# Layer 1's scan on one core: odd pairs mirrored, two chains taking turns product by product, v's projection in pieces of six products

## The chip, the core and the metric

The kernel runs on one core of a Trainium2 chip. The metric is the device time of one execution in microseconds. TensorE (PE in the profile) multiplies and writes PSUM; VectorE (DVE) and ScalarE (ACT) read PSUM and do elementwise work; GpSimd (POOL) does elementwise work in SBUF; SyncE's queue (SP) issues DMAs.

## The reference, cut to what matters

The program is a trunk of two layers on 512 tokens of width 2048, in float32. Layer 0 is attention and a pooling mixer; the change leaves its arithmetic alone. Layer 1 is RWKV-7 time mixing with 32 heads of 64:

```python
def step(state, inp):
    r_t, w_t, k_t, v_t, kk_t, a_t = inp
    sa = jnp.einsum('bhvk,bhk->bhv', state, -kk_t)
    state = (state * w_t[:, :, None, :]
             + sa[..., None] * (kk_t * a_t)[:, :, None, :]
             + v_t[..., None] * k_t[:, :, None, :])
    return state, jnp.einsum('bhvk,bhk->bhv', state, r_t)
```

This recurrence runs over the 512 tokens for each head. Before it stand the projections of r, k, v and the gate; after it a group norm, the gate and the output projection.

## The kernel before, in words

The recurrence is worked in chunks of 64 tokens, 8 chunks for each head. Two heads make a pair `p`, 16 pairs in all, one head on partitions 0 to 63 and the other on 64 to 127. Ahead of the scan, `prep` (L756) writes for each pair the scaled vectors to DRAM: `AR` (per chunk 64 columns of "a", 64 of "r") and `BK` (per chunk 64 columns of "b", 64 of "k").

`scan` (L814) holds generators, one for each kind of work on one pair; a `next` issues one piece.

- `vproj` (L844): v's projection for the pair, 16 steps of three products 128x128 by 512 (`mm3`, L140, lines 142 to 144 in the profile, output `vps`), then a copy on ACT. It yields after each step: 16 pieces.
- `gprod` (L863): the chunk's products of BK and AR, masked by DVE into two tiles `Z` (L882), and the transposed BK in `BT`: 6 pieces.
- `lanes` (L912, 18 pieces, DVE almost alone: a serial inversion in blocks of 16, L928 and L929) and `levels` (L947, 5 pieces, four of which hold products, L963 and L973) make the chunk's inverse `U`. `vprep` (L892) fills `RS` with v, `post` (L1035, 6 pieces) is the group norm; its DVE line L1054 must be done before its transposes on PE, L1058.
- `chain` (L992): the serial part, 8 chunks of three steps. Step one: `xo` gets AR times the state M (L1002, one product with 128 output rows for "a" and "r" at once; the first chunk has none) and, on the 64 "a" rows, Z times RS for each head (L1004); DVE (L1006) and ACT (L1007) copy the a rows to `xs`. Step two: `sa` = U times xs (L1010, 64 output rows); DVE copies it to RS (L1011). Step three: `s1` = BT times RS (L1017, one head on the lower 64 output rows, one on the upper), from which DVE makes the next state M (L1026, L1028, two operations); then Z times RS on the 64 "r" rows of xo (L1030), which ACT copies to the output O (L1031).

In every pair "a" stands on the lower 64 output rows (`lo`) and "r" on the upper 64 (`hi`). A product whose output has 64 rows uses one half of TensorE's columns, lower or upper; all of these use all 128 rows of the array. A float32 product runs as two passes, so the profile counts two instructions for each call.

The order of TensorE's work is written by hand (L753); other engines are ordered by the framework. `slot` (L1117) runs two chains side by side, one pair in its last four chunks and the next pair in its first four: 12 rounds a slot, and in a round each chain gives one step, then come the pieces of other work that are due:

```python
for q in range(12):
    for c in chains:
        with tc.high_priority(offset=400):
            next(c)
    while todo and todo[0][0] < at + q + 1:
        next(todo.pop(0)[2])
```

`plan` (L1115) gives the pieces of each generator evenly spaced due times between two bounds (L31, in rounds). For slots 0 to 12 this makes one pattern of 12 rounds. By the bounds, v's 16 pieces fall on twelve rounds, ten of them alone and three times two in a row; gprod's products on rounds 0, 1, 3, 4, 6 and 7; levels' products on rounds 5, 7, 9 and 10; post's transposes on round 5, vprep's on round 11. Slot -1 holds one chain and slot 15 one; from the middle of slot 13 on v's pieces are gone, and pieces of the output projection (`project`, L1095, lines 488 to 490, output `y`) take their place.

Of the kernel before, what the change touches and what calls it, by code (L numbers as in the profile page):

```python
# [17 lines left out]
P = 128  # L18
# [16 lines left out]
class Kernel:  # L35
# [488 lines left out]
    def consts1(self, cp, tp):  # L524
        nc = self.nc
        f = lambda n, w=P: tp.tile([P, w], F32, name="c1" + n)

        mk = self.mk = cp.tile([P, P], F32, name="mk")
        nc.gpsimd.memset(mk, 1.0)
        nc.gpsimd.affine_select(mk[:64, :64], mk[:64, :64], [[1, 64]], ALU.is_gt, 0.0, base=0, channel_multiplier=-1)  # L530
        nc.gpsimd.affine_select(mk[:64, 64:], mk[:64, 64:], [[1, 64]], ALU.is_ge, 0.0, base=0, channel_multiplier=-1)
        nc.vector.tensor_copy(mk[64:, :], mk[:64, :])
# [223 lines left out]
    def prep(self, tp, p, r, hid, k_d, rn_d, ar_d, bk_d, bc_d):  # L756
# [35 lines left out]
        nc.vector.scalar_tensor_tensor(rn, k, col(self.hv["kk"]), rn, ALU.mult, ALU.mult)  # L792
        nc.vector.scalar_tensor_tensor(AR[:, :, 0, :], c8(rn), -2.0, Pi[:, :, 0:64], ALU.mult, ALU.mult)
        nc.vector.tensor_mul(AR[:, :, 1, :], c8(r), Pi[:, :, 1:])
        nc.sync.dma_start(ar_d[p], AR.rearrange("p a b c -> p (a b c)"))
        nc.vector.scalar_tensor_tensor(rn, ta, 1.0, rn, ALU.add, ALU.mult)
        nc.vector.tensor_mul(BK[:, :, 0, :], c8(rn), c8(iP))
        nc.scalar.activation(ta, ta, AF.Identity, scale=col(self.hv["ka"]), bias=col(self.hv["oka"]))
        nc.vector.tensor_mul(k, k, ta)
        nc.vector.tensor_mul(BK[:, :, 1, :], c8(k), c8(iP))  # L800
        nc.sync.dma_start(bk_d[p], BK.rearrange("p a b c -> p (a b c)"))
# [12 lines left out]
    def scan(self, ctx, xv, first, mp, ld, ar_d, bk_d, bc_d, g_d, m_d):  # L814
# [29 lines left out]
        def vproj(p):  # L844

            unit = lambda k0: self.wunit(
                Wv[k0 * P:(k0 + 4) * P, p * P:(p + 1) * P].rearrange("(k p) n -> p k n", p=P), 4, P,
                eng=nc.gpsimd if p > 1 else None)
            ws = first if p == 0 else [unit(0)]
            ps = pv.tile([P, S], F32, tag="v", name="vps")  # L850
            for k in range(NK):
                if k % 4 == 0:
                    wh, wl = ws.pop(0)
                    if k + 4 < NK and not ws:
                        ws.append(unit(k + 4))
                self.mm3(ps, wh[:, k % 4, :], wl[:, k % 4, :], xv[k][:, 0, :], xv[k][:, 1, :], k == 0, k == NK - 1)
                if k < NK - 1:
                    yield
            vT = sets[p]["vT"] = tp.tile([P, S], F32, tag="vT", name="vT")
            nc.scalar.copy(vT, ps)  # L860
            yield

        def gprod(p):  # L863
# [9 lines left out]
            for b in range(2):  # L873
# [7 lines left out]
                for h in range(2):  # L881
                    nc.vector.tensor_mul(Z[h][:, 4 * b:4 * b + 4, :], g[h], self.mk.unsqueeze(1).to_broadcast([P, 4, P]))  # L882
                yield
# [8 lines left out]
        def vprep(p):  # L892
# [6 lines left out]
            RS = s["RS"] = st.tile([P, 8, 2, 64], F32, tag="RS", name="RS", bufs=3)  # L899
            nc.gpsimd.memset(RS[lo], 0.0)  # L900
            yield
# [4 lines left out]
            for par, rows in ((0, lo), (1, hi)):  # L906
                nc.scalar.copy(RS[hi, par::2], g5[rows])
            yield
# [3 lines left out]
        def lanes(p):  # L912

            for q in range(4):
                r, c = slice(32 * q, 32 * q + 32), slice(32 * (q % 2), 32 * (q % 2) + 32)
                nc.gpsimd.tensor_mul(nd2[r, :, :16].rearrange("p t (b c) -> p c b t", b=2),
                                     sets[p]["Z"][q // 2][c, :, c].rearrange("p c (b t) -> p c b t", b=2),
                                     self.md[c, c].rearrange("p (b t) -> p b t", b=2)
                                     .unsqueeze(1).to_broadcast([32, 8, 2, 16]))
# [27 lines left out]
        def levels(p):  # L947
# [5 lines left out]
            N1 = tp.tile([P, 8, 64], F32, tag="N1", name="N1")  # L953
            nc.scalar.copy(N1[hi], sets[p]["Z"][1][lo, :, :64])
            N = sets[p]["Z"][0], N1
            yield
# [35 lines left out]
        def chain(p):  # L992

            s = sets[p]
            AR, RS, U, BT, Z = (s[n] for n in ("AR", "RS", "U", "BT", "Z"))
            O = s["O"] = tp.tile([P, 4, 2, 64], F32, tag="O", name="O", bufs=3)
            M = None
            for c in range(8):

                xo = pc.tile([P, 2, 64], F32, tag="c", name="xo")  # L1000
                if c:
                    mm(xo, AR[:, c].rearrange("p a b -> p (a b)"), M, start=True, stop=False)  # L1002
                for h in range(2):
                    mm(xo[lo, h, :], Z[h][:, c, :64], RS[:, c, h, :], start=c == 0 and h == 0, stop=h == 1)  # L1004
                xs = xsb[p % 2]
                nc.vector.tensor_copy(xs[lo, 0, :], xo[lo, 0, :])  # L1006
                nc.scalar.copy(xs[hi, 1, :], xo[lo, 1, :])  # L1007
                yield
                sa = po.tile([64, 2, 64], F32, tag="o", name="sa")
                mm(sa, U[:, c, :], xs, start=True, stop=True)  # L1010
                nc.vector.tensor_copy(RS[lo, c], sa)  # L1011
                yield
                Mn = None
                if c < 7:
                    s1 = po.tile([P, 64], F32, tag="o", name="s1")
                    for h in range(2):
                        mm(s1[half[h], :], BT[:, c, 64 * h:64 * h + 64], RS[:, c, h, :], start=True, stop=True)  # L1017
                    Mn = Ms[p % 2 * 2 + c % 2]
                    if c:
                        m0 = tp.tile([P, 2, 64], F32, tag="m0", name="m0", bufs=2)  # L1020
                        nc.scalar.activation(m0, M, AF.Copy, scale=self.pcs[:, p, c:c + 1])
                    for h in range(2):
                        hh = half[h]
                        pC = self.pcs[hh, p, c:c + 1]
                        if c:
                            nc.vector.scalar_tensor_tensor(Mn[hh, h, :], s1[hh, :], pC, m0[hh, h, :], ALU.mult, ALU.add)  # L1026
                        else:
                            nc.vector.tensor_scalar(Mn[hh, h, :], s1[hh, :], pC, None, ALU.mult)  # L1028
                for h in range(2):
                    mm(xo[hi, h, :], Z[h][:, c, 64:], RS[:, c, h, :], start=c == 0 and h == 0, stop=h == 1)  # L1030
                nc.scalar.copy(O[half[c % 2], c // 2], xo[hi])  # L1031
                M = Mn
                yield

# [84 lines left out]
        def slot(at, chains):  # L1119

            todo.sort(key=lambda x: x[0])
            for q in range(12):
                for c in chains:
                    with tc.high_priority(offset=400):
                        next(c)
                while todo and todo[0][0] < at + q + 1:
# [9 lines left out]
        def plan_pair(base, q, skip=0):  # L1136
# [11 lines left out]
        next(gp)  # L1148
        for q in range(7):
            next(v)  # L1150
        run(gp)
        la = lanes(0)
        for q in range(16):
            next(la)
            next(v, None)
        g1, v = gprod(1), vproj(1)
        next(g1)
        run(la)
        for q in range(6):
            next(g1)  # L1160
            next(v)
        run(vprep(0))
        la, l0 = lanes(1), levels(0)
        for q in range(10):
            if q % 2 == 0:
                next(l0, None)
            if q < 6:
                next(la)
            next(v)
        run(l0)  # L1170
# [115 lines left out]
```

## Time and profile before

| what | value |
|---|---|
| median of three runs | 2153.81 us |
| lowest and highest | 2153.8 and 2154.24 us |
| the profiled execution | 2158.38 us |
| its span, first to last instruction | 2156.7 us |
| mean granted TensorE clock (1 is 2.4 GHz) | 0.989 |

The profile is of one execution; 1.7 us of its time lie outside its span. The scan runs from about 1467 us to 1985 us of the span; slot 0 begins at 1490.5 us. A line of the timeline gives the start of the first instruction of a run of like ones, the time until the last of them ends, the engine, the line, out and in, rows and columns of the array (as 128*64), the operands and the count. Matmul ends are modelled and overlap; what a run of products costs is the distance from its start to the start of the next.

### The profile page before, as it was taken

To read this page: it belongs to the slowest core of one execution; us is meant where nothing else is said; L and a number is where in the kernel's file an instruction comes from. 1 tells how busy PE (TensorE), PEld (TensorE's weight loads), DVE (VectorE), ACT (ScalarE), POOL (GpSimd) and SP (SyncE) were. 2 spreads that over 40 slices of the span, in tenths; PEclk is the share of its full clock that TensorE was granted. 3 is DMA by queue.
4 is the path that set the end of the run, shared out by engine and by line. 5 is a ranking of instruction groups with operands and counts; after the bars stand their busy time and mean duration, and the time that the engine had idled before them with its cause. 6 is when DMAs were issued, how large, how long until landed. Compare 5 with 4: busy or idle time off the path is not lost.

```text
span 2156.7 us, 33268 instructions
## 1 busy us (share of the span) xinstructions
PE 2087.6 (97%) x12915; PEld 1688.5 (78%) x12915; DVE 1272.0 (59%) x2557; ACT 951.8 (44%) x1663; POOL 266.1 (12%) x333
## 2 busy tenths in 40 slices
PE   8999999999999989998999989999999999999997
PEld 7888888888888888777788768876777777767786
DVE  4334335444333368677767872276787877876346
ACT  3335435333221248455545662254555555554211
POOL 0000000000000000233000020022233233210003
PEclk9999999999999999999999999999999999999998
DMA  5322222333333353554466664321232332232633
GB/s 189 98 70 81 85 73 69 93 98 98 98 108 114 127 175 112 165 165 149 159 209 223 219 226 152 107 84 45 89 99 81 93 104 77 91 118 89 229 103 112
DMA packets 214029, 262.94 MB, mean 122 GB/s; under 512 B 15768, under 2 KB 161776, under 8 KB 213104
## 3 DMA queue, kind: packets, MB, share of 16 engines
q1 hardware_dynamic: 213872, 260.83, 37.6%
q8 instruction: 101, 1.65, 0.3%
q14 instruction: 56, 0.46, 0.1%
HBM read 214.32 MB, written 46.47 MB: 121 GB/s over the span
## 4 chain that ended last, share of the span: by engine, by line
PE 82%; DVE 9%; DMA 4%; ACT 2%; issue 1%; POOL 1%; SPq 0%; DVEq 0%; ACTq 0%
PE ga L142 14%; PE ga L144 13%; PE ga L143 13%; PE gb L488 4%; PE gb L490 4%; PE gb L489 4%; PE vps L142 4%; PE vps L143 2%; PE vps L144 2%; PE xo L1004 2%; PE sa L1010 2%; PE g L877 2%; PE xo L1002 2%; DVE wlo L138 1%; PE xo L1030 1%
## 5 line engine op out<-in xcount | busy, mean ns | idle before, releaser
L138 DVE TENSOR_TENSOR wlo<-wraw,whi 128x1024 fp32r<-128x1024 f32 (+1 forms) x268 | 313.0, 1170 | 491.0 <-ACT whi L137 476.6
L137 ACT CAST whi<-wraw 128x1024 fp32r<-128x1024 f32 (+1 forms) x324 | 303.6, 939 | 643.5 <-PE ga L143 310.5
L142 PE MATMUL ga<-mx,whi 128*128 128x512 f32 x768 | 301.3, 393 | 5.6 <-ACT mx L137 5.6
L143 PE MATMUL ga<-mx,whi 128*128 128x512 f32 x768 | 302.0, 393 | 3.8 <-DVE mx L138 3.8
L144 PE MATMUL ga<-mx,wlo 128*128 128x512 f32 x768 | 301.4, 392 | 0.0
L142 PE MATMUL ga<-x,whi 128*128 128x512 f32 x768 | 301.2, 392 | 0.0
L144 PE MATMUL ga<-x,wlo 128*128 128x512 f32 x768 | 299.6, 390 | 0.3 <-DVE wlo L138 0.3
L143 PE MATMUL ga<-x,whi 128*128 128x512 f32 x768 | 299.3, 390 | 0.0
L490 PE MATMUL gb<-wlo,mixed 128*128 128x512 f32 (+1 forms) x576 | 197.6, 344 | 4.3 <-DVE wlo L138 4.3
L488 PE MATMUL gb<-whi,mixed 128*128 128x512 f32 (+1 forms) x576 | 198.1, 344 | 2.9 <-DVE s L439 2.9
L489 PE MATMUL gb<-whi,mixed 128*128 128x512 f32 (+1 forms) x576 | 197.6, 343 | 0.0
L142 PEld LDWEIGHTS ga<-mx,whi 128*128 128x128 f32 x768 | 145.4, 189 | 39.1 <-ACT mx L137 7.2
L143 PEld LDWEIGHTS ga<-mx,whi 128*128 128x128 f32 x768 | 145.4, 189 | 37.3 <-DVE mx L138 6.0
L144 PEld LDWEIGHTS ga<-mx,wlo 128*128 128x128 f32 x768 | 145.4, 189 | 30.8 <-issue 0.3
L144 PEld LDWEIGHTS ga<-x,wlo 128*128 128x128 f32 x768 | 144.2, 188 | 31.1 <-DVE wlo L138 0.8
L142 PEld LDWEIGHTS ga<-x,whi 128*128 128x128 f32 x768 | 144.4, 188 | 29.4 <-ACT whi L137 0.3
L143 PEld LDWEIGHTS ga<-x,whi 128*128 128x128 f32 x768 | 144.5, 188 | 29.1
L490 PEld LDWEIGHTS gb<-wlo,mixed 128*128 128x128 f32 x576 | 109.4, 190 | 18.2 <-DVE wlo L138 5.5
L488 PEld LDWEIGHTS gb<-whi,mixed 128*128 128x128 f32 x576 | 109.6, 190 | 17.3 <-DVE s L439 4.6
L142 PE MATMUL vps<-mx,whi 128*128 128x512 f32 x256 | 121.1, 473 | 0.3 <-ACT vT L860 0.3
L489 PEld LDWEIGHTS gb<-whi,mixed 128*128 128x128 f32 x576 | 109.6, 190 | 12.5
L138 POOL TENSOR_TENSOR wlo<-wraw,whi 128x512 fp32r<-128x512 f32 x56 | 73.7, 1316 | 241.3 <-ACT whi L137 187.4
(331 smaller groups left out, 3499.3 us busy)
## 6 DMA issues: line engine op xcount, KB each, us to landing
wraw<-in_ev_w_in SPq DMA_DIRECT2D x96, 512.0 KB, 3.5
wraw<-in_ev_w_out SPq DMA_DIRECT2D x32, 512.0 KB, 3.6
wraw<-in_od_w_k SPq DMA_DIRECT2D x32, 512.0 KB, 4.5
wraw<-in_od_w_r SPq DMA_DIRECT2D x32, 512.0 KB, 4.1
wraw<-in_od_w_g SPq DMA_DIRECT2D x32, 512.0 KB, 3.5
wraw<-in_od_w_v SPq DMA_DIRECT2D x64, 256.0 KB, 2.8
ar_d<-pAR SPq DMA_DIRECT2D x16, 512.0 KB, 2.6
bk_d<-pBK SPq DMA_DIRECT2D x16, 512.0 KB, 3.3
```

Of the source, the lines that this page charges most:

```text
L137: self.nc.scalar.copy(hi, src)
L138: (eng or self.nc.vector).tensor_sub(lo, src, hi.bitcast(F32))
L142: mm(ps, ah, bh, start=start, stop=False)
L143: mm(ps, ah, bl, start=False, stop=False)
L144: mm(ps, al, bh, start=False, stop=stop)
L488: mm(ps, ah, bh, start=start, stop=False)
L489: mm(ps, al, bh, start=False, stop=False)
L490: mm(ps, ah, bl, start=False, stop=stop)
L877: mm(g[h][:, c, :], BK[half[h], 4 * b + c, :], AR[half[h], 4 * b + c].rearrange("p a b -> p (a b)"), start=True, stop=True)
L1002: mm(xo, AR[:, c].rearrange("p a b -> p (a b)"), M, start=True, stop=False)
L1004: mm(xo[lo, h, :], Z[h][:, c, :64], RS[:, c, h, :], start=c == 0 and h == 0, stop=h == 1)
L1010: mm(sa, U[:, c, :], xs, start=True, stop=True)
```

## The change

It does three things. In odd pairs "a" and "r" are exchanged: a on the upper 64 rows, r on the lower, in AR, BK, the masks, Z, RS, U's inputs and xo. `chain` yields more often: `False` after each part of a step, `True` at its end, and a round goes through the two chains by turns until each has said `True`; the product of AR and the state is split in two of 64 output rows. And `vproj` yields after every second step, so that there are 8 pieces of six products; the stretch ahead of slot -1 hands them out at every second opportunity.

```diff
-        mk = self.mk = cp.tile([P, P], F32, name="mk")
+        mk = self.mk = cp.tile([P, 192], F32, name="mk")
...
+        for c, op in ((0, ALU.is_gt), (64, ALU.is_ge), (128, ALU.is_gt)):
+            nc.gpsimd.affine_select(mk[:64, c:c + 64], mk[:64, c:c + 64], [[1, 64]], op, 0.0, base=0, channel_multiplier=-1)
...
-        nc.vector.scalar_tensor_tensor(AR[:, :, 0, :], c8(rn), -2.0, Pi[:, :, 0:64], ALU.mult, ALU.mult)
-        nc.vector.tensor_mul(AR[:, :, 1, :], c8(r), Pi[:, :, 1:])
+        ia, ir = p % 2, 1 - p % 2
+        nc.vector.scalar_tensor_tensor(AR[:, :, ia, :], c8(rn), -2.0, Pi[:, :, 0:64], ALU.mult, ALU.mult)
+        nc.vector.tensor_mul(AR[:, :, ir, :], c8(r), Pi[:, :, 1:])
...
-                if k < NK - 1:
+                if k % 2 and k < NK - 1:
                     yield
...
-            nc.scalar.copy(N1[hi], sets[p]["Z"][1][lo, :, :64])
-            N = sets[p]["Z"][0], N1
+            Z, own, odd = sets[p]["Z"], p % 2, 64 * (p % 2)
+            nc.scalar.copy(N1[half[1 - own]], Z[1 - own][half[own], :, odd:odd + 64])
+            N = [N1, N1]
+            N[own] = Z[own][:, :, odd:odd + 64]
...
+            own = p % 2
+            a, r = half[own], half[1 - own]
...
                 if c:
-                    mm(xo, AR[:, c].rearrange("p a b -> p (a b)"), M, start=True, stop=False)
+                    for h in range(2):
+                        mm(xo[half[h]], AR[:, c, h, :], M, start=True, stop=False)
+                yield False
                 for h in range(2):
-                    mm(xo[lo, h, :], Z[h][:, c, :64], RS[:, c, h, :], start=c == 0 and h == 0, stop=h == 1)
-                xs = xsb[p % 2]
-                nc.vector.tensor_copy(xs[lo, 0, :], xo[lo, 0, :])
-                nc.scalar.copy(xs[hi, 1, :], xo[lo, 1, :])
-                yield
-                sa = po.tile([64, 2, 64], F32, tag="o", name="sa")
-                mm(sa, U[:, c, :], xs, start=True, stop=True)
-                nc.vector.tensor_copy(RS[lo, c], sa)
-                yield
+                    mm(xo[a, h, :], Z[h][:, c, a], RS[:, c, h, :], start=c == 0 and h == 0, stop=h == 1)
+                    if h == 0:
+                        yield False
+                xs = xsb[own]
+                nc.vector.tensor_copy(xs[a, own, :], xo[a, own, :])
+                nc.scalar.copy(xs[r, 1 - own, :], xo[a, 1 - own, :])
+                yield True
+                sa = po.tile([P, 2, 64], F32, tag="o", name="sa")
+                mm(sa[a], U[:, c, :], xs, start=True, stop=True)
+                nc.vector.tensor_copy(RS[a, c], sa[a])
+                yield True
...
+                yield False
                 for h in range(2):
-                    mm(xo[hi, h, :], Z[h][:, c, 64:], RS[:, c, h, :], start=c == 0 and h == 0, stop=h == 1)
-                nc.scalar.copy(O[half[c % 2], c // 2], xo[hi])
+                    mm(xo[r, h, :], Z[h][:, c, r], RS[:, c, h, :], start=c == 0 and h == 0, stop=h == 1)
+                    if h == 0:
+                        yield False
+                nc.scalar.copy(O[half[c % 2], c // 2], xo[r])
                 M = Mn
-                yield
+                yield True
...
             for q in range(12):
-                for c in chains:
-                    with tc.high_priority(offset=400):
-                        next(c)
+                live = list(chains)
+                with tc.high_priority(offset=400):
+                    while live:
+                        live = [c for c in live if not next(c)]
...
-            plan(base, vproj(q), 16, *VJ)
+            plan(base, vproj(q), 8, *VJ)
```

## Rows read from the trace of the kernel before

**Rows 1.** The page: busy time, share of the span, instructions.

```profile
PE 2087.6 (97%) x12915; PEld 1688.5 (78%) x12915; DVE 1272.0 (59%) x2557; ACT 951.8 (44%) x1663; POOL 266.1 (12%) x333
```

**Rows 2.** Windows: length, busy PE, PEld, DVE, ACT, POOL; clock, DMA share, GB/s.

```profile
1492.98:1908.12 415.14, 413.64 (x4487) 310.16 (x4486) 327.83 (x1106) 220.76 (x563) 133.85 (x130) 1.00 0.30 91
1588.54:1620.51 31.97, 31.97 (x347) 23.90 (x346) 25.26 (x87) 16.95 (x44) 10.33 (x10) 1.00 0.30 92
```

**Rows 3.** Timeline of PE: step one, both chains past their first chunk.

```profile
1601.42 0.39 PE L1002 MATMUL xo<-M,AR 128*128 128x128 f32 x2
1601.74 0.45 PE L1004 MATMUL xo<-RS,Z 128*64 128x64 f32 x4
...
1602.91 0.66 PE L888 MATMUL bt<-ident,BK 128*128 128x128 f32 x4
```

**Rows 4.** Timeline of PE: step one where the second chain starts, then gprod.

```profile
1618.06 0.38 PE L1002 MATMUL xo<-M,AR 128*128 128x128 f32 x2
1618.37 0.68 PE L1004 MATMUL xo<-RS,Z 128*64 128x64 f32 x8
1618.98 0.72 PE L877 MATMUL g<-AR,BK 64*128 64x128 f32 x8
```

**Rows 5.** Timeline of PE: the third step in round 11, then vprep's transposes.

```profile
1615.44 0.27 PE L1030 MATMUL xo<-RS,Z 128*64 128x64 f32 x1
1615.46 0.27 PE L1017 MATMUL s<-RS,BT 128*64 128x64 f32 x1
1615.55 0.22 PE L1030 MATMUL xo<-RS,Z 128*64 128x64 f32 x1
1615.56 0.22 PE L1017 MATMUL s<-RS,BT 128*64 128x64 f32 x1
1615.61 0.28 PE L1030 MATMUL xo<-RS,Z 128*64 128x64 f32 x2
...
1616.17 0.66 PE L904 MATMUL vt<-ident,vT 128*128 128x128 f32 x4
```

**Rows 6.** Timeline of PE: the third step in round 8, its beginning and what follows.

```profile
1607.60 0.34 PE L1017 MATMUL s<-RS,BT 128*64 128x64 f32 x4
...
1608.45 0.50 PE L142 MATMUL vps<-mx,whi 128*128 128x512 f32 x1
```

**Rows 7.** Timeline of PE: two pieces of v in a row, then step two.

```profile
1603.32 0.48 PE L142 MATMUL vps<-mx,whi 128*128 128x512 f32 x1
...
1604.89 0.65 PE L1010 MATMUL sa<-xs,U 128*64 128x128 f32 x4
1605.47 0.91 PE L973 MATMUL c<-U,q1z 64*48 64x32 f32 x32
```

**Rows 8.** Timeline of PE: one piece of v alone, then step two.

```profile
1612.46 0.50 PE L142 MATMUL vps<-mx,whi 128*128 128x512 f32 x1
...
1613.35 0.65 PE L1010 MATMUL sa<-xs,U 128*64 128x128 f32 x4
```

**Rows 9.** Timeline of DVE: the copies of step two, both chains.

```profile
1613.82 0.50 DVE L1011 COPY RS<-sa 64x128 f32<-64x128 f32 x2 [0.73 <-PE sa L1010]
```

**Rows 10.** Timeline of DVE, round 8: the state's updates of both chains.

```profile
1608.46 0.97 DVE L1026 SCALAR_TENSOR_TENSOR M<-s,pcs,m 64x64 f32<-64x64 f32 x4
```

**Rows 11.** Timelines of DVE and PE: post's last scaling and the transposes that need it.

```profile
1629.71 0.69 DVE L1054 TENSOR_TENSOR O<-O,rsygn 128x512 f32<-128x512 f32 x1
...
1632.91 0.66 PE L1058 MATMUL ot<-ident,O 128*128 128x128 f32 x4
```

**Rows 12.** Slot 13: the same transposes late, and the window (as rows 2) around.

```profile
1920.65 1.12 PE L1058 MATMUL ot<-ident,O 128*128 128x128 f32 x4 [2.49 <-DVE O L1054]
...
1919.87:1926.69 6.82, 6.04 (x23) 4.31 (x23) 2.61 (x7) 2.42 (x5) 0.23 (x1) 0.50 0.46 155
```

**Rows 13.** Start of the span: the mask on POOL; the first weights (chain of waits).

```profile
1.70 0.23 POOL L531 TENSOR_SCALAR_AFFINE_SELECT mk<-mk 64x64 f32<-64x64 f32 x1
...
1.86 8.42 DMA wraw<-in_ev_w_in
```

More of the change, by code (lines that the diff above doesn't have):

```diff
@@ L526, in consts1 @@
         f = lambda n, w=P: tp.tile([P, w], F32, name="c1" + n)
-        mk = self.mk = cp.tile([P, P], F32, name="mk")
+        mk = self.mk = cp.tile([P, 192], F32, name="mk")
         nc.gpsimd.memset(mk, 1.0)
-        nc.gpsimd.affine_select(mk[:64, :64], mk[:64, :64], [[1, 64]], ALU.is_gt, 0.0, base=0, channel_multiplier=-1)
-        nc.gpsimd.affine_select(mk[:64, 64:], mk[:64, 64:], [[1, 64]], ALU.is_ge, 0.0, base=0, channel_multiplier=-1)
+        for c, op in ((0, ALU.is_gt), (64, ALU.is_ge), (128, ALU.is_gt)):
+            nc.gpsimd.affine_select(mk[:64, c:c + 64], mk[:64, c:c + 64], [[1, 64]], op, 0.0, base=0, channel_multiplier=-1)
         nc.vector.tensor_copy(mk[64:, :], mk[:64, :])
@@ L792, in prep @@
         nc.vector.scalar_tensor_tensor(rn, k, col(self.hv["kk"]), rn, ALU.mult, ALU.mult)
-        nc.vector.scalar_tensor_tensor(AR[:, :, 0, :], c8(rn), -2.0, Pi[:, :, 0:64], ALU.mult, ALU.mult)
-        nc.vector.tensor_mul(AR[:, :, 1, :], c8(r), Pi[:, :, 1:])
+        ia, ir = p % 2, 1 - p % 2
+        nc.vector.scalar_tensor_tensor(AR[:, :, ia, :], c8(rn), -2.0, Pi[:, :, 0:64], ALU.mult, ALU.mult)
+        nc.vector.tensor_mul(AR[:, :, ir, :], c8(r), Pi[:, :, 1:])
         nc.sync.dma_start(ar_d[p], AR.rearrange("p a b c -> p (a b c)"))
         nc.vector.scalar_tensor_tensor(rn, ta, 1.0, rn, ALU.add, ALU.mult)
-        nc.vector.tensor_mul(BK[:, :, 0, :], c8(rn), c8(iP))
+        nc.vector.tensor_mul(BK[:, :, ia, :], c8(rn), c8(iP))
         nc.scalar.activation(ta, ta, AF.Identity, scale=col(self.hv["ka"]), bias=col(self.hv["oka"]))
         nc.vector.tensor_mul(k, k, ta)
-        nc.vector.tensor_mul(BK[:, :, 1, :], c8(k), c8(iP))
+        nc.vector.tensor_mul(BK[:, :, ir, :], c8(k), c8(iP))
         nc.sync.dma_start(bk_d[p], BK.rearrange("p a b c -> p (a b c)"))
@@ L881, in gprod @@
                 for h in range(2):
-                    nc.vector.tensor_mul(Z[h][:, 4 * b:4 * b + 4, :], g[h], self.mk.unsqueeze(1).to_broadcast([P, 4, P]))
+                    mk = self.mk[:, 64 * (p % 2):64 * (p % 2) + P]
+                    nc.vector.tensor_mul(Z[h][:, 4 * b:4 * b + 4, :], g[h], mk.unsqueeze(1).to_broadcast([P, 4, P]))
                 yield
@@ L899, in vprep @@
             RS = s["RS"] = st.tile([P, 8, 2, 64], F32, tag="RS", name="RS", bufs=3)
-            nc.gpsimd.memset(RS[lo], 0.0)
+            nc.gpsimd.memset(RS[half[p % 2]], 0.0)
             yield
@@ L906, in vprep @@
             for par, rows in ((0, lo), (1, hi)):
-                nc.scalar.copy(RS[hi, par::2], g5[rows])
+                nc.scalar.copy(RS[half[1 - p % 2], par::2], g5[rows])
             yield
@@ L915, in lanes @@
                 r, c = slice(32 * q, 32 * q + 32), slice(32 * (q % 2), 32 * (q % 2) + 32)
+                b = slice(64 * (p % 2) + c.start, 64 * (p % 2) + c.stop)
                 nc.gpsimd.tensor_mul(nd2[r, :, :16].rearrange("p t (b c) -> p c b t", b=2),
-                                     sets[p]["Z"][q // 2][c, :, c].rearrange("p c (b t) -> p c b t", b=2),
-                                     self.md[c, c].rearrange("p (b t) -> p b t", b=2)
+                                     sets[p]["Z"][q // 2][b, :, b].rearrange("p c (b t) -> p c b t", b=2),
+                                     self.md[b, c].rearrange("p (b t) -> p b t", b=2)
                                      .unsqueeze(1).to_broadcast([32, 8, 2, 16]))
@@ L1017, in chain @@
                         mm(s1[half[h], :], BT[:, c, 64 * h:64 * h + 64], RS[:, c, h, :], start=True, stop=True)
-                    Mn = Ms[p % 2 * 2 + c % 2]
+                    Mn = Ms[own * 2 + c % 2]
                     if c:
@@ L1148, in scan @@
         next(gp)
-        for q in range(7):
+        for q in range(3):
             next(v)
@@ L1154, in scan @@
             next(la)
-            next(v, None)
+            if q % 2:
+                next(v, None)
         g1, v = gprod(1), vproj(1)
@@ L1160, in scan @@
             next(g1)
-            next(v)
+            if q % 2:
+                next(v)
         run(vprep(0))
@@ L1168, in scan @@
                 next(la)
-            next(v)
+            if q % 2:
+                next(v)
         run(l0)
```

## The prediction

> **What bounds the kernel now.** I read the shares first: TensorE is busy 97% of the span, VectorE 59% [rows 1]. An average hides stages, so the windows come next, over the scan alone. Slots 0 to 12 take 415.14 us, 31.93 each, and in one of them PE is busy for the whole 31.97 us while DVE is busy 25.26, which leaves DVE idle for 6.71 [rows 2]. So PE sets the pace, and DVE, at 79%, is the nearest rival. "Busy" says nothing of how well PE is used, since the modelled ends overlap; so I read its timeline and took each run of products from its start to the next start.
>
> Step one of a round takes 1.49 us: for each chain an AR product, then four Z passes [rows 3]. Where the second chain is at its first chunk it takes .92 [rows 4]. Step two takes .58 for both chains [rows 7]. Step three takes .85 [rows 6] and, in round 11, where one chain has no state to make, .73 [rows 5].
>
> Two prices are in these rows. A pass of 64 columns on one half of the array follows the last at .06 us (1615.55 to 1615.61), a pass of 128 at about .11. And the two halves run side by side: the first passes of L1030 and L1017, on different halves, start at 1615.44 and 1615.46, their second passes at 1615.55 and 1615.56 [rows 5]. In round 11 the upper half has ten passes, the lower two: ten at .058 are .58, and .15 is left for the change to the next kind of product. In the full step the upper half has twelve: .70 and .15 make the .85 measured [rows 6]. With the sixteen one after another it would be .93 and .15.
>
> **The change, part by part.** All per slot of twelve rounds, four of each step.
>
> Step one. Now all passes of both chains' Z use the lower half, and AR the whole array. After, each AR product is two of 64 rows, one in each half: each half gets four passes of .107 (.43) and, with the chains mirrored, two heads of one chain, four of .058 (.23). With .145 at the end that is .81 against 1.49, .68 less, in three rounds. The fourth has one chain's AR: .21+.23+.145=.59 against .92, .33 less. Together 2.37.
>
> Step two. Two passes of .107 in each half instead of four in one: .21 less, four times: .84.
>
> Step three. The halves go from four and twelve passes to eight each: .46+.15=.61 against .85; in round 11 from two and ten to six each: .24 less both times, four rounds: .96.
>
> v's projection. A piece alone takes .89 to the next start [rows 8], two in a row 1.57 [rows 7]: .19 and .17 beyond the passes, so the loss is by the piece. Ten single and three double pieces are 8.9+4.6 (the other two doubles ran at about 1.49)=13.4; eight double ones at 1.57, all of which now stand before a product on half the array, 12.56: .88 less. Its four weight loads a pair stay, each asked for at the same step, with SP's queue passed in the same order.
>
> PE's sum: 2.37+.84+.96+.88=5.05 us a slot, which leaves 26.9.
>
> **What comes late then.** In a 26.9 us slot DVE's 25.26 us are 94%. Two places get short cover. First, the copies after step two: they start .47 after step two does and both are over at .97 (1613.35 to 1613.82 and .50 more) [rows 8, 9]. The .89 pieces of v that covered this leave rounds 1, 4, 7 and 10; in 1, 4 and 10 one gprod or levels piece is left, some .65 (gprod's is .72 with the tail of its last pass [rows 4]), in 7 two. After step two's .37 the third step would start at 1.02, just as the copies end, and any DVE operation in the way delays it. The bounds are nothing, if DVE is free as in [rows 9], and one of its long operations, .69 [rows 11]. I take .3, the middle, three times: .9 a slot. Second, taking turns queues a chain's Z products behind the other chain's AR, which waits for that chain's state. DVE makes all four updates in .97 [rows 10], over 1.83 after step three began [rows 6, 10]; step one follows at .61+1.57=2.18 or later. I cost this at nothing, covered by the .35 between; if a long operation came first it would be some .35, inside the bound below. For the whole slot, waits have the bounds 0 and 1.8.
>
> The rest. The third mask piece on POOL costs .23 beside the first weight load, which takes 8.42 us [rows 13]: nothing, unless that load were gone, and then .23. The exchanged indices in prep, gprod, lanes, levels and vprep leave their counts and shapes. The stretch ahead of slot -1 has fewer changes for v, but waits for lanes on DVE: nothing. Slot -1 is only partly PE's: -.5 of the .88. Slot 13 would lose 4.5 on PE, but already waits 2.49 us for post's scaling [rows 12], which a faster PE only reaches sooner: -2. Slot 14 has y pieces after each step and no v: 4.17 less .7 for waits, -3.5. Slot 15 loses one change in four rounds, -.4.
>
> Sum: 13 slots at 5.05-.9=4.15 give 54; with .5, 2, 3.5 and .4, 60.4. The profiled execution took 2158.38 us, so 2098 on its own time; the median of the runs shown is 4.6 lower, and there the forecast is **2093**. About 0.2% (4 us) is what a measurement of this kernel can tell from no change.
>
> **A rule against the change.** The halves' overlap carries most of the sum, and the row for it is the pair of starts .02 apart [rows 5], with weights from all 128 rows on both sides. The Trainium skill (TensorE: Matmul & The Clock Gate, Part 3: Packing small matmuls — row/col tiling, under what overlaps and what doesn't) says that a weight load overlaps running matmuls only when they use other row groups, and that matmuls keep program order. By that rule halves that share all rows would gain nothing from turns, and the sum would be rival C's; by the rows it is the sum above. Here trace and page differ, and I go by the trace.
>
> **Rivals.** A: DVE takes over. Its order is fixed, and it idles where the next operation waits for PE. If of its 6.71 us idle 4.5 stay, a slot is 29.8, 2.1 less: 13 times that and 3 more give 2123. For it: the 94%, and post's scaling, done at 1630.40 for transposes at 1632.91, a slack of 2.5 us when PE moves 5 us nearer [rows 11]. Against: DVE's waits are for PE's results, which come sooner too.
>
> B: that slack runs out in every slot as in slot 13. There PE waits 2.49, then the granted clock is .50 (1.2 GHz) for 6.82 us [rows 12]: with .78 of the wait inside it, half of 6.04, or 3.0, is lost. 2.5+3.0 eats the 5.05: 13 times +.45, less the other slots' 6, is about 2153, no change.
>
> C, slower: the turns cost. If products of different halves did not overlap and each began with its weights uncovered (first to second pass .11 against .06, .05 a product), step one would be 4 AR products of .26, 4 Z of .17 and .145: 1.87, +.38 three times, and 1.34 in the fourth, +.42; step two +.09 four times; step three 8 times .17 and .15, +.62 three times, and +.41: 4.2 a slot, less .88 for v. Thirteen times 3.3 and two slots of 4.2 are +51: 2205. It turns on whether the second chain's first passes start before the first chain's are over. [Rows 5] speak against it.
>
> D: more. The waits of .9 stay hidden (12 us) and a long piece of v costs 1.49 instead of 1.57 (13 slots of .64, 8): about 2073, and 2068 with some of slot 13's wait gone. That the change doesn't do what it says I rule out: PE runs in the order written, as the eight Z passes of two chains before gprod in [rows 4] show.
>
> **The numbers.** Forecast, waits between 0 and 1.8 a slot, 2078 to 2106: .62. A, 2106 to 2140: .22. D: .09. B: .03. C: .04. The range 2068 to 2126 leaves out B, C, the far part of A and a little of D, some .16. Faster .93, same .03, slower .04.
>
> **What would show it.** In the profile after: L1002 as 128*64 with both halves starting together, step one near .8, two of 0.37, three of .6, half as many changes into v; slots near 27.8, DVE over 88% busy in them, and new PE waits for RS (L1017) in rounds 1, 4 and 10. Wrong would be: Z passes of the two chains in single file; PE waits at L1058 or L963 with the clock at .50; slots over 29 us with DVE full.

## The result, and the profile after

The changed kernel takes **2135.82 us** (median; 2133.68 to 2138.29), the kernel before 2153.81 (2151.38 to 2154.24) on the same chip: a ratio of .9908, 95% interval .9892 to .9924. It is faster by .9%, 18 us of the 60 forecast, and lies outside the range of the prediction (2068 to 2126).

The page first: busy time, share of the span and instructions.

```profile
PE 2036.6 (96%) x13139; PEld 1645.7 (77%) x13139; DVE 1301.0 (61%) x2557; ACT 954.4 (45%) x1663; POOL 268.9 (13%) x334
```

PE's busy time fell by 51 us against [rows 1], DVE's rose by 29 with the same 2557 instructions. The windows, columns as in [rows 2], of slots 0 to 12, of slot 13 and of slot 14:

```profile
1487.09:1887.99 400.90, 373.32 (x4669) 277.44 (x4668) 351.77 (x1100) 222.57 (x560) 135.95 (x130) 1.00 0.30 93
1887.99:1918.38 30.39, 24.20 (x305) 17.06 (x305) 24.93 (x72) 18.20 (x47) 1.28 (x1) 0.89 0.32 105
1918.38:1940.46 22.08, 20.50 (x179) 13.40 (x179) 18.42 (x51) 12.17 (x34) 0.00 (x0) 1.00 0.39 126
```

A slot takes 400.90/13 = 30.84 us instead of 31.93. PE is busy for 373.32 of the 400.90, where before it was busy for all but 1.5 of 415.14 [rows 2]; DVE for 351.77, 27.06 a slot, against 327.83, 25.22 a slot. So DVE's idle time fell from 6.72 us a slot to 3.78, and DVE is at 88%.

PE's products did become shorter. Its timeline, steps one, two and three of the changed kernel where nothing holds them up:

```profile
1620.32 0.66 PE L1014 MATMUL xo<-M,AR 128*64 128x128 f32 x8
1620.80 0.40 PE L1017 MATMUL xo<-RS,Z 128*64 128x64 f32 x8
1621.13 0.66 PE L891 MATMUL bt<-ident,BK 128*128 128x128 f32 x4
1621.55 0.48 PE L142 MATMUL vps<-mx,whi 128*128 128x512 f32 x1
...
1623.12 0.44 PE L1025 MATMUL sa<-xs,U 128*64 128x128 f32 x4
1623.49 0.91 PE L980 MATMUL c<-U,q1z 64*48 64x32 f32 x32
...
1624.91 0.45 PE L1032 MATMUL s<-RS,BT 128*64 128x64 f32 x8
1625.19 0.40 PE L1046 MATMUL xo<-RS,Z 128*64 128x64 f32 x8
1625.53 0.50 PE L142 MATMUL vps<-mx,whi 128*128 128x512 f32 x1
```

Step one takes .81 us (1620.32 to 1621.13), step two .37, step three .62, a piece of v 1.57 (1621.55 to 1623.12). These are the best cases. Of the 39 full ones of either kind in slots 0 to 12, step one takes .82 in 18 and .91 to 1.43 in the others, step three .61 to .67 in 19 and .80 to .82 in 20. What PE gained it waits away. The waits of slots 0 to 12 (total us, times, longest us), PE's and DVE's:

```profile
DVE lt L925 <- POOL nd L920: 22.2, 13, 2.7
PE s L1032 <- DVE RS L1026: 21.2, 25, 1.7
DVE RS L1026 <- PE sa L1025: 3.4, 5, 2.1
PE c L970 <- ACT q L991: 2.6, 6, 1.0
PE xo L1014 <- DVE M L1041: 1.3, 4, 0.6
DVE xs L1021 <- PE xo L1017: 1.0, 1, 1.0
```

DVE's longest waits in the kernel before:

```profile
DVE xs L1006 <- PE xo L1004: 31.3, 45, 1.6
DVE RS L1011 <- PE sa L1010: 11.6, 19, 1.7
DVE U L943 <- ACT DT L939: 10.2, 12, 1.1
DVE lt L921 <- POOL nd L916: 8.7, 13, 1.1
```

The wait for step one's product went from 31.3 us to 1.0, that for step two's from 11.6 to 3.4, that for DT from 10.2 to .7: DVE hardly waits for PE any more, and PE waits for DVE's RS copy. What grew is DVE's wait at lt, the transpose at the head of `lanes`, for the masked blocks nd that GpSimd makes: 1.71 us a slot.

The rise in DVE's busy time has a pattern of its own. A stretch of the timeline:

```profile
1638.09 0.30 DVE L933 TENSOR_REDUCE uc<-pr 128x12 f32<-128x144 f32 x1
1638.19 1.26 POOL L138 TENSOR_TENSOR wlo<-wraw,whi 128x512 fp32r<-128x512 f32 x1 [4.23 <-ACT whi L137]
1638.31 1.17 DVE L207 TENSOR_SCALAR rshgn<-gs 128x8 f32<-128x8 f32 x1
1639.52 0.61 DVE L1026 COPY RS<-sa 64x128 f32<-64x128 f32 x2
...
1639.86 0.65 PE L1032 MATMUL s<-RS,BT 128*64 128x64 f32 x8 [1.25 <-DVE RS L1026]
```

An operation of DVE on 128x8 elements stands for 1.17 us. It begins just after GpSimd's wlo (the low part of a weight tile of v, 128x512) and ends .03 us after it; the RS copies come behind it, and PE waits 1.25. In slots 0 to 12, 33 operations of DVE (L932 pr, L207 rshgn, L1069 gs) stood over .3 us longer than usual in this way, each ending .02 to .25 us after one of GpSimd's, 32 of them after a wlo; in the kernel before, 15.

### The profile page after: what moved, and what is told of

The parts are those of the page before. It is cut to its first block, busy times and chain, and to the rows that moved or that the text cites. A ratio compares the mean times of both kernels' runs of the same rounds, so it can differ in the third digit from the quotient of the medians.

```text
span 2132.1 us, 33773 instructions
## 1 busy us (share of the span) xinstructions
PE 2036.6 (96%) x13139; PEld 1645.7 (77%) x13139; DVE 1301.0 (61%) x2557; ACT 954.4 (45%) x1663; POOL 268.9 (13%) x334
## 5 line engine op out<-in xcount | busy, mean ns | idle before, releaser
L142 PE MATMUL vps<-mx,whi 128*128 128x512 f32 x256 | 113.3, 443 | 0.0
```

Source lines behind the costliest of these rows:

```text
L142: mm(ps, ah, bh, start=start, stop=False)
```

## The experiments

Three questions: is DVE's order the bound, what are the long operations, and what does each part of the change earn? The expectations weigh two theories. By the first ("full DVE") a slot waits for the whole line of DVE's work; by the second ("short cover") only the copies of step two come late, because too little of PE's work is left to cover them.

The tables give the median, the ratio to the kernel before with its interval, and for slots 0 to 12 the slot's length as DVE's busy plus idle time. Each ratio is against runs of the kernel before beside it (medians 2154.2 to 2155.8). Times that differ by a few us say less than the slots do: the profiled execution of the changed kernel reached the chains' first product at 1461.5 us, that of the kernel without turns at 1469.5, though the two differ only in what comes after it.

| run | us | ratio (95%) | slot = DVE busy + idle |
|---|---|---|---|
| before | 2153.81 | 1 | 31.93 = 25.22 + 6.72 |
| after | 2135.82 | .9908 (.9892 to .9924) | 30.84 = 27.06 + 3.78 |

### Is DVE the bound?

In two kernels the loop of `lanes` is left out (the 15 products and sums that make U), so that DVE has less to do and PE has the same:

```diff
-            pr = tp.tile([P, 16, 16], F32, tag="i5", name="pr")
             yield
             for t in range(1, 16):
-                q = pr[:, :t, :t]
-                nc.vector.tensor_mul(q, uc[:, :t, :t], la[:, t, :t].unsqueeze(1).to_broadcast([P, t, t]))
-                nc.vector.tensor_reduce(uc[:, :t, t], q, AX.X, ALU.add)
                 yield
```

From the changed kernel:

> The changed kernel without the serial inversion (the loop of L932 and L933 in lanes; the inverse of each block of 16 is left out). Full-DVE theory: VectorE fills the changed slot (27.06 us busy, 1.6 of short gaps, 2.2 of waits in 30.84). The loop holds 8.1 us of it a slot, so without it the slot falls to what TensorE needs, 26.9, and the time to about 2080 (2070 to 2095). Short-cover theory: the third step waits for the copies of step two because nothing covers them, which does not depend on how much else VectorE has to do: the slot stays over 30 and the time over 2120.

From the kernel before:

> The kernel before without the same loop (L928 and L929). Both theories: TensorE filled its slot, so taking 8 us a slot from VectorE gives next to nothing: slots 31.6 to 31.9, time 2140 to 2154, the few us from slot 13 and the stretch ahead of the scan. If it fell under 2130, VectorE would have been a bound before too, and the experiment on the changed kernel would say less.

| run | us | ratio (95%) | slot = DVE busy + idle |
|---|---|---|---|
| after, no loop | 2091.32 | .9706 (.9689 to .9722) | 28.35 = 20.59 + 7.76 |
| before, no loop | 2145.0 | .9952 (.9935 to .9969) | 31.71 = 19.00 + 12.71 |

The windows of slots 0 to 12, the changed kernel without the loop, and the kernel before without it:

```profile
1482.96:1851.51 368.55, 362.67 (x4669) 271.53 (x4669) 267.66 (x722) 222.87 (x562) 132.84 (x130) 1.00 0.33 102
```

```profile
1487.43:1899.67 412.24, 412.11 (x4487) 310.61 (x4487) 247.01 (x723) 219.81 (x564) 133.65 (x130) 1.00 0.30 92
```

The same work taken off DVE is worth 44.5 us in the changed kernel and 8.8 in the one before (43.5 and 10.3 by the ratios). That is shown: the change made DVE the bound. PE's waits in the changed kernel are for the RS copy and not for what the loop makes, so it is not a wait for the loop's result that goes. With the loop gone PE is busy for 362.67 of 368.55. The time comes within 2 us of the forecast, but the slot, 28.35, is still .55 over the forecast's 27.8.

### What holds DVE's short operations?

GpSimd's wlo is taken away: the low parts of v's weights are left out from the third pair on (the high part stands in for them, so PE has the same number of products), in the changed kernel and in the one before.

```diff
         hi = pool.tile([P, ww], F32R, tag="whi", name="whi", **kw)[:, :a * b].rearrange("p (a b) -> p a b", a=a)
+        if eng is not None:
+            self.nc.scalar.copy(hi, raw)
+            return hi, hi
```

> The changed kernel with the low parts of v's weights left out from the third pair on (GpSimd's four operations of 1.33 us a slot; the third product of each step takes the high part instead). GpSimd theory: VectorE's short operations that stand for a microsecond (1.3 us a slot over their usual length) do so while GpSimd works, and go with half of GpSimd's work: 0.7 to 1.2 us a slot, 2118 to 2127. If GpSimd's work costs VectorE nothing: 2130 to 2140.

> The kernel before with the low parts of v's weights left out from the third pair on, as in e12. VectorE theory: TensorE was the bound and did not wait for GpSimd, so shorter holds of VectorE are worth little: 2144 to 2156. If TensorE waited for the low parts, the gain of e12 (25 us) shows here too: under 2135.

In a third kernel nothing is left out; GpSimd makes each low part in four operations of 128x128 instead of one:

```diff
-        (eng or self.nc.vector).tensor_sub(lo, src, hi.bitcast(F32))
+        if eng is None:
+            self.nc.vector.tensor_sub(lo, src, hi.bitcast(F32))
+        else:
+            for n in range(4):
+                eng.tensor_sub(lo[:, n], src[:, n], hi.bitcast(F32)[:, n])
```

> The changed kernel with each of GpSimd's subtractions for the low parts of v's weights (128x512, 1.33 us) issued as four of 128x128; nothing is left out. If a GpSimd operation holds off VectorE's until it ends, a hit now costs at most about 0.4 us instead of up to 1.3: VectorE's busy time falls by 0.6 to 1.2 us a slot and the time to 2118 to 2128. If the run without the low parts gained because TensorE no longer waited for them, four operations with their own starts are no earlier: 2132 to 2142.

| run | us | ratio (95%) | slot = DVE busy + idle |
|---|---|---|---|
| after, no low part | 2110.79 | .98 (.9783 to .9816) | 28.85 = 25.24 + 3.61 |
| before, no low part | 2153.42 | .9996 (.9984 to 1.0008) | 31.82 = 24.71 + 7.12 |
| after, low part in four | 2120.33 | .9836 (.9814 to .9858) | 29.33 = 25.64 + 3.69 |

The operations by line over slots 0 to 12 (busy, mean ns | idle before). The changed kernel:

```profile
L932 DVE TENSOR_TENSOR pr<-uc,la 128x1 f32<-128x1 f32 (+4 forms) x191 | 61.4, 321 | 4.3
L933 DVE TENSOR_REDUCE uc<-pr 128x1 f32<-128x1 f32 (+4 forms) x190 | 44.3, 233 | 3.9
L207 DVE TENSOR_SCALAR rshgn<-gs 128x8 f32<-128x8 f32 x12 | 6.5, 544 | 0.0
```

Without the low parts (its lines stand three further down):

```profile
L935 DVE TENSOR_TENSOR pr<-uc,la 128x1 f32<-128x1 f32 (+4 forms) x191 | 46.9, 246 | 4.4
L936 DVE TENSOR_REDUCE uc<-pr 128x1 f32<-128x1 f32 (+4 forms) x191 | 44.5, 233 | 3.8
L210 DVE TENSOR_SCALAR rshgn<-gs 128x8 f32<-128x8 f32 x12 | 1.9, 160 | 0.0
```

With the low part in four:

```profile
L936 DVE TENSOR_TENSOR pr<-uc,la 128x1 f32<-128x1 f32 (+4 forms) x191 | 51.6, 270 | 4.3
L142 POOL TENSOR_TENSOR wlo<-wraw,whi 128x128 fp32r<-128x128 f32 x208 | 93.6, 480 | 203.3 <-ACT whi L137 184.4 <-DVE RS L1030 18.9
```

rshgn goes from 544 to 160 ns and pr from 321 to 246, while the reduce stays at 233: the two operations that read only SBUF and are no reduce were held, the reduce was not. PE's wait for the RS copy falls to this (without the low parts):

```profile
PE s L1035 <- DVE RS L1029: 6.9, 14, 0.8
```

So the holds are GpSimd's, 1.82 us of DVE a slot, and they cost the changed kernel 25 us, more than the 9 to 18 expected, and the kernel before .4, inside its interval: there DVE's idle time took them up. That is also what tells them from a wait of PE for wlo itself, which would have shown in the kernel before; nor does the changed kernel's list of waits have one. Cut in four, GpSimd's work takes longer (4 times .48 us against 1.26 above), yet 1.42 of the 1.82 come back and 15 us with them: here it counts how long one operation of GpSimd lasts, and not how long all of them do. The Trainium skill (SBUF — State Buffer, Who interferes with whom) says that VectorE and GpSimd share a port pair under a lock that one of them keeps for its whole instruction, and that reduces on this chip don't contend; these rows agree, 160 ns against 544 for the one and 233 against 233 for the other.

With both taken off DVE, the loop of `lanes` and the low parts left out, and the transpose lt issued behind the last xs copy (below), the changed kernel should run at PE's pace:

> The changed kernel without the inversion's loop and without the low parts (both left out), lt behind the copies to xs: VectorE has some 18 us of work a slot. If the prediction's sum for TensorE is right, slots are 27.0 to 27.9 and the time 2070 to 2085. If the slot stays at the 28.35 of the run without the loop alone, the sum was short by more than a microsecond a slot: 2088 to 2094.

It took 2084.41 us (.968, .9652 to .9708); the window of slots 0 to 12:

```profile
1485.12:1844.36 359.24, 357.27 (x4669) 270.17 (x4669) 257.51 (x720) 222.24 (x562) 66.88 (x78) 1.00 0.34 104
```

27.63 us a slot, and PE is busy for 357.27 of 359.24, 27.48 a slot. The forecast's slot was 27.8, of which 26.9 PE's work.

### What does each part of the change earn?

**Turns.** Each chain goes through its whole step before the other one begins:

```diff
             for q in range(12):
-                live = list(chains)
-                with tc.high_priority(offset=400):
-                    while live:
-                        live = [c for c in live if not next(c)]
+                for c in chains:
+                    with tc.high_priority(offset=400):
+                        while not next(c):
+                            pass
```

> The changed kernel, mirrored and with long pieces of v, but each chain gives its whole step before the other. Full-DVE theory: whatever TensorE loses up to 3 us a slot is covered: 2130 to 2145. If turns are what makes the halves overlap, step one rises from .82 to 1.2 or more in the profile and step two stays .37; if the queue overlaps them by itself, step one stays under .95. If the waiting in turns was a cost (a chain's products behind the other's wait), the time falls to 2120 or less.

The same with the loop of `lanes` left out, so that DVE is no bound:

> The run without turns, and without the serial inversion's loop (left out as in the first run), so that VectorE is not what the slot waits for. If turns earn something on TensorE (step one .82 against .88, step three .62 against .78 without them), this is 0.8 us a slot and 8 to 12 us slower than the changed kernel without the loop (2091): 2099 to 2103. If the waiting in turns costs more than the overlap earns even there, 2085 or less. If neither matters, 2088 to 2094.

| run | us | ratio (95%) | slot = DVE busy + idle |
|---|---|---|---|
| after, no turns | 2126.81 | .9854 (.983 to .9878) | 29.77 = 25.91 + 3.86 |
| no turns, no loop | 2097.38 | .9735 (.9717 to .9752) | 28.43 = 19.87 + 8.55 |

Without turns the kernel is 9 us faster, between the two outcomes expected. PE's timeline of step one there:

```profile
1619.52 0.44 PE L1014 MATMUL xo<-M,AR 128*64 128x128 f32 x4
1619.79 0.34 PE L1017 MATMUL xo<-RS,Z 128*64 128x64 f32 x3
1619.91 0.32 PE L1014 MATMUL xo<-M,AR 128*64 128x128 f32 x1
1619.96 0.22 PE L1017 MATMUL xo<-RS,Z 128*64 128x64 f32 x1
1620.02 0.39 PE L1014 MATMUL xo<-M,AR 128*64 128x128 f32 x3
1620.17 0.40 PE L1017 MATMUL xo<-RS,Z 128*64 128x64 f32 x4
1620.50 0.71 PE L879 MATMUL g<-AR,BK 64*128 64x128 f32 x8
```

The second chain's AR passes begin at 1619.91, between the first chain's Z passes. With the pairs mirrored PE overlaps the halves though the products stand one chain after the other: step one takes .98 in these lines (1619.52 to 1620.50), .88 in 18 rounds of 39 and .93 in the mean, against .82 with turns where nothing is late and 1.49 before; step two .37 both ways. So mirroring by itself brings most of the overlap, though no run has it without the larger pieces of v. With the loop left out, turns shorten steps one and three by .39 us a slot (5.87 against 6.26), but the products c and g take .29 longer with them (4.28 against 3.99), and the slot is only .08 shorter (28.35 against 28.43). The time without turns is 6 us longer there (2097.38 against 2091.32), again between two of the outcomes expected; in the profiles 1.0 of that lies in slots 0 to 12 and 6.8 ahead of them, where no turns are taken. Where DVE is the bound, the slot is 1.07 shorter without turns, and DVE's busy time 1.15 (27.06 to 25.91). By line, over the 13 slots, 4.2 us less stand at pr and 3.1 at gs, operations that GpSimd holds, and 4.3 less at the state's updates (L1041, 39.5 against 43.8), though a single update lasts as long (278 ns in the mean, 281 with turns): without turns some overlap, as the four that took .97 in [rows 10]. So what the slot gains lies on DVE, half of it in holds; why fewer are held was not tried.

**v's pieces.** Sixteen of three products in the changed kernel (`if k < NK - 1: yield` and `plan(base, vproj(q), 16, *VJ)`, and the stretch ahead as it was), and eight of six in the kernel before:

> The changed kernel with v's projection in 16 pieces of three products as before, mirrored pairs and turns kept. Full-DVE theory: TensorE has time to spare in the slot, so the 0.9 us a slot that long pieces saved on it are worth nothing: 2128 to 2142, as the changed kernel. By TensorE's sum alone: 14 times 0.9 more, 2146 to 2150. Short-cover theory: rounds 1, 4 and 10 get their cover back: 2110 to 2125.

> The kernel before with v's projection in 8 pieces of six products, pairs and chains as before. TensorE's sum: it was the bound there, so 0.9 a slot is gained, 14 times: 2138 to 2147. Full-DVE theory agrees, since a slot of 31 still leaves VectorE 4 us. Short-cover theory: here too rounds 1, 4 and 10 are left short, and the gain is given back: 2150 to 2160.

| run | us | ratio (95%) | slot = DVE busy + idle |
|---|---|---|---|
| after, v in 16 | 2158.4 | 1.0016 (.9997 to 1.0035) | 32.43 = 27.32 + 5.11 |
| before, v in 8 | 2150.63 | .9979 (.9965 to .9993) | 31.73 = 26.95 + 4.78 |

In the kernel before, the larger pieces earn 3 us, where the forecast's term of .88 a slot alone would be 11: DVE's busy time grew to 26.95, and .20 a slot came out of it. Its growth is pr's, 303 ns in the mean before (58.3 us over the 13 slots) and now

```profile
L928 DVE TENSOR_TENSOR pr<-uc,la 128x1 f32<-128x1 f32 (+14 forms) x192 | 82.8, 431 | 3.2
```

so the larger pieces alone already make holds: 45 operations of DVE in these slots, counted as above, against 15. In the changed kernel the small pieces cost 22.6 us, more than any reading gave. PE's waits there (columns as above) show where:

```profile
PE ot L1076 <- DVE O L1072: 13.4, 6, 2.3
PE xo L1014 <- DVE M L1041: 13.1, 29, 1.6
```

and the granted clock over the 13 slots is .96:

```profile
1490.07:1911.70 421.63, 392.17 (x4669) 280.82 (x4669) 355.18 (x1100) 222.65 (x562) 136.19 (x130) 0.96 0.29 89
```

So PE waits for post's scaling and for the state, and its clock is lower in part of the time. Why small pieces put the work of DVE in that order stays open.

**Reliefs that leave nothing out.** The pieces of v put back where they cover step two's copies:

```diff
-            plan(base, vproj(q), 8, *VJ)
+            g = vproj(q)
+            for at in (5, 7, 8, 10, 11, 13, 14, 16):
+                plan(base, g, 1, at + 0.5, 0)
```

> The changed kernel with v's eight pieces put on rounds 1, 2, 4, 5, 7, 8, 10 and 11, so that each step two is followed by 1.6 us more work for TensorE, none on rounds 0, 3, 6 and 9. Full-DVE theory: nothing is taken from VectorE; 2130 to 2140, as the changed kernel. Short-cover theory: the waits for RS in rounds 1, 4, 10 (47 us with weight loads counted, in 13 slots) go, slots near 28, time 2095 to 2105.

It took 2153.98 us (.9994, .9979 to 1.0008; slot 32.10 = 26.57 + 5.53), slower than the changed kernel and outside what both theories expected. The waits for RS are gone, and another has their place:

```profile
PE sa L1025 <- ACT xs L1022: 34.9, 47, 2.1
```

Cover moved to one copy is missing at the other. RS is copied by ScalarE instead:

```diff
-                nc.vector.tensor_copy(RS[a, c], sa[a])
+                nc.scalar.copy(RS[a, c], sa[a])
```

> The changed kernel with step two's copies (L1026, eight a slot) on ScalarE. Full-DVE theory: VectorE loses 2.3 us a slot and the wait of third steps behind its queue goes: slots 28.5 to 29.3, time 2105 to 2118. Short-cover theory: the copies take as long on ScalarE and start as late, so rounds 1, 4 and 10 stay uncovered: 2128 to 2140. A third outcome, slower than the changed kernel, would mean that ScalarE's queue, which stands for microseconds at its weight casts, holds the copies.

2125.55 us (.9861, .9846 to .9876; slot 30.23 = 26.43 + 3.80), between the two ranges: 2.31 us of copies leave DVE, but its busy time falls by .63 only. About half of the difference is that more of what is left is held by GpSimd (pr +.78, gs +.37, rshgn -.34 a slot). The transpose lt, where DVE waits for GpSimd's nd, is issued behind the last xs copy:

```diff
+        last_xs = [None]
...
-            nc.vector.transpose(lt.rearrange("p a b -> p (a b)"), nd2.rearrange("p a b -> p (a b)"))
+            with tc.issue_after(last_xs[0].ins) if last_xs[0] else ExitStack():
+                nc.vector.transpose(lt.rearrange("p a b -> p (a b)"), nd2.rearrange("p a b -> p (a b)"))
...
-                nc.vector.tensor_copy(xs[a, own, :], xo[a, own, :])
+                last_xs[0] = nc.vector.tensor_copy(xs[a, own, :], xo[a, own, :])
```

> The changed kernel with the transpose lt (L925) ordered on VectorE behind step one's copies to xs; now VectorE stands at it 1.7 us a slot until GpSimd's four masked pieces are ready, with those copies queued behind. Full-DVE theory: VectorE's standing time is worth as much as its work: 1.0 to 1.7 a slot, 2113 to 2124. Short-cover theory: the waits for RS stay, step two merely comes earlier to them: 2128 to 2140.

2135.75 us (.9903, .9875 to .9931; slot 30.58): nothing by itself, against what the full-DVE theory expected. DVE no longer stands at lt, but 1.59 us a slot for the xs copy's input instead. The reliefs together, without turns: RS on ScalarE, then lt too, then the low part in four as well:

> Mirrored pairs and long pieces of v, no turns, and step two's copies on ScalarE. Full-VectorE theory: 2.3 us of work leave VectorE in a slot of 29.8, and the two gains (10 and 9 us) add for the most part: 2108 to 2119. If both only removed the same wait of third steps for RS, the sum is no better than the better one: 2122 to 2128.

> The same with the transpose lt behind step one's copies. By the earlier run of that alone nothing is gained: within 4 us of the run without it. If VectorE's standing at lt counts once step two's copies are gone from its queue, 5 to 12 us less: 2098 to 2110.

> No turns, step two's copies on ScalarE, lt behind the copies to xs, and the subtractions in four. In the run without the split VectorE still had GpSimd's holds (1.2 us a slot by the same count at most): 2103 to 2113 by the first theory, 2114 to 2122 by the second.

| run | us | ratio (95%) | slot = DVE busy + idle |
|---|---|---|---|
| no turns, RS on ScalarE | 2121.52 | .9851 (.9836 to .9867) | 29.79 = 25.72 + 4.07 |
| and lt behind xs | 2116.25 | .9829 (.9807 to .9851) | 29.45 = 24.40 + 5.05 |
| and the low part in four | **2112.11** | .9803 (.9777 to .9829) | 28.83 = 23.16 + 5.67 |

The first lies between its two outcomes: its gain and that of leaving out turns add only in part (14 us of 19). The second is 5 us faster than the first, the least that was to show that the standing at lt counts, but the two intervals overlap. The third lies in the range expected; it computes everything and is faster than both kernels, by 42 us and by 24.

## Why the prediction was wrong, point by point

**PE's prices were right where nothing is late.** Step one .81 forecast and .81 measured (.88 to .98 without turns); step two .37 and .37; step three .61 and .62, though .67 in the mean even with DVE relieved; a double piece of v 1.57 and 1.57 to 1.59 [rows 3 to 8]. With DVE relieved the slot is 27.63, where 26.9 and waits of .9 had given 27.8. That the two agree is in part luck: PE is busy for 27.48 of it, .6 more than its sum, and waits .15. The chains' steps and v's pieces gave back 4.82 us of the 5.05; the products bt, ot, c and g, which the sum left as they were, take .54 more (5.81 against 5.27). Rival C, products of both halves in single file, is contradicted by the second chain's start at 1619.91, before the first chain's passes are over. What the prediction worked out by the rule of the Trainium skill (TensorE: Matmul & The Clock Gate, Part 3) does not come out in these traces: step one costs .81 with all 128 rows behind both halves, not rival C's 1.87.

**The waits were in the right place.** PE's new wait is for the RS copy: 21.2 us in 13 slots, 1.6 each, for which I took .9 between 0 and 1.8. But they are the symptom: the copies are late because DVE's line ahead of them is, and covering them moved the wait (34.9 us at xs).

**The step that failed** is "In a 26.9 us slot DVE's 25.26 us are 94%": it takes DVE's busy time as all that DVE needs and its 6.71 us of idle time as free. In its place the runs put two terms. First, some idle time stays when DVE is the bound: 3.61 us a slot without the low parts, 3.78 with. In the changed kernel 1.6 of it are gaps, most of them of about .03 us, between its 85 operations, and 2.2 waits, 1.71 of them at lt for nd. Without the low parts the slot is 25.24+3.61 = 28.85, 1.07 over the forecast's 27.78. Second, GpSimd's holds add 1.99 to the slot (30.84 less 28.85). Together 3.06, 13 times 40 us: 2093 and 40 are 2133, against 2135.82.

**Rival A** had the side and the band (2106 to 2140), at .22. Its arithmetic was another: it let 4.5 us of idle stay and held the busy time at 25.26, 29.8; in fact less idle stayed, and the busy time grew by 1.84. GpSimd's low parts cost DVE 1.82 in the changed kernel and .51 in the one before (25.22 less 24.71), where they were part of the 25.26 that I took as fixed. The other .53 stand without low parts too (25.24 against 24.71): there the RS copies take 30.0 us of the 13 slots against 25.2 and the state's updates 43.8 against 40.2, though a single copy lasts 289 ns against 275 and an update 281 against 280, so that they overlapped before and no longer do. The argument against A, that DVE's waits are for PE's results, held for those waits (42.9 us in the 13 slots before, 4.4 after); it left out the wait at lt for GpSimd, which grew from 8.7 to 22.2. The sign "slots over 29 us with DVE full" stood in the prediction, and it is what the windows show.

**The smaller terms.** Slot 13 gained 1.07 for 2 forecast: PE's wait for post's scaling went from 2.49 [rows 12] to 2.8. Slot 14 gained 1.06 for 3.5. Its waits in the changed kernel add to 1.59, against .7 allowed:

```profile
1927.60 0.66 PE L1076 MATMUL ot<-ident,O 128*128 128x128 f32 x4 [0.98 <-DVE O L1072]
...
1935.11 0.67 PE L1025 MATMUL sa<-xs,U 128*64 128x128 f32 x4 [0.45 <-ACT xs L1022]
1935.71 0.50 PE L488 MATMUL y<-wo,mixed 128*128 128x512 f32 x1
...
1936.83 0.34 PE L1032 MATMUL s<-RS,BT 128*64 128x64 f32 x4 [0.16 <-DVE RS L1026]
```

The step two in these lines takes .60 instead of .37. With the 2.44 missing from slot 14 and .93 from slot 13 the sum above comes to 2136. Slot -1 became .09 shorter, for .5 forecast, and slot 15 gained nothing for .4: from its start to the chain's last product 19.9 us, 19.5 before. Two sums of the prediction are a little off: by its prices rival C's third step is 1.51, .66 more and not .62, and waits between 0 and 1.8 a slot give 2082 to 2105 by themselves, where it has 2078 to 2106; neither changes an outcome. The mask and the exchanged indices showed no cost.

## What to carry to other kernels

When the busiest engine is about to be made faster, add to the next engine's busy time the gaps and the in-order waits that it can't lose (here 3.6 to 3.8 us in 85 operations), and set the sum against the new pace; a share of 79% left only 3 of the 6.7 us. Look for that engine's operations that are long for their size and end with an operation of another engine: such holds are hidden while it has idle time and cost their full length when it hasn't (.4 us and 25 us here). And mirror two chains onto the halves of the array first: the hardware overlapped them by itself, and an order written by hand beside it can cost more than it earns.

## What was not expected of the hardware

A 128x8 operation of VectorE took 160 ns alone and 544 in the mean beside GpSimd's 1.26 us operations, and four operations of .48 us on GpSimd hurt less than one of 1.26. Taking work off VectorE (the RS copies, 2.31 us a slot) brought back a quarter of it; about half of the rest went into more holds. And VectorE's operations can overlap: 156 state updates of 278 ns each fill 39.5 us without turns, of 281 ns 43.8 us with them. And products that share all 128 rows, on different column halves, ran side by side in program order of either kind, .81 us with turns and .88 to .98 without, for 1.49 before.
